# Inverses of the RWKV chunks applied ahead in batches, and a credit for small products, in a one-layer hybrid decoder step

## The chip, the cores and the metric

The kernel runs on one core of a Trainium2 chip. The metric is device time in microseconds (us) of one execution. TensorE (PE in the profile) multiplies, VectorE (DVE) and ScalarE (ACT) do elementwise work and empty PSUM, GpSimd (POOL) does little here, and SyncE (SP) issues most DMAs. The program is written with a tile framework: it records the operations, places the tiles in memory, sets the semaphores and orders each engine's instructions by a plan of its own. Around the part that is changed here, the order on PE is not the framework's: the kernel writes it out itself.

## The reference

One step of one layer: RWKV-7 time mixing beside dilated window attention, for a prompt of 1024 tokens and for 8 x 4 sample tokens. In outline:

```python
h = x @ w_in                                 # 1024 -> 9344 columns: r,k,v,lora | gates | q,k,v | branch gates
# RWKV-7, 8 heads of 64; per token t and head:
#   sa = S @ (-kk_t);  S = S * w_t + sa (kk_t*a_t)^T + v_t k_t^T;  o_t = S @ r_t
# attention: 3 groups (window 128/512/2048, dilation 1/4/16) x 4 heads x 128, merged by their softmax sums
mix = sigmoid(g_r) * (y_r @ w_oa) + sigmoid(g_a) * (y_a @ w_ob)
y = layer_norm(ALPHA * x + mix @ w_out)
```

Outputs are y, the new keys and values, the final RWKV states and the last projected rows.

## The kernel before

All large products are made in float32r with the operands split into a high and a low part, three matmuls for one. A projection of 128 columns (`project_steps`, its matmuls are L172) multiplies 2 halves of the inner dimension x 3 pieces of 352 tokens x 12 matmuls, 72 in all, into three PSUM banks of a pool `pj` that has four. A `consume` function then empties each bank. Weights come in halves by DMA (`wraw`), ACT makes the high part (`whi`, L162) and DVE the low part (`wlo`, L163).

The program has these stages. First x is transposed and the lora columns are projected. Then comes the RWKV stage, from some 75 us to some 600 us, which holds 12 projections for r, k and v and 23 of `fill`: gates whose results wait in DRAM (`zd`, `gd`). After it comes attention with its 36 projections, the first of them for the values (V, tile `v`), keys and queries of the first head; and then the two branch products and the last product with its layer norm.

The RWKV recurrence is worked in chunks of 64 tokens. A unit is a pair of heads (j) and half of the prompt (hf), so there are eight units of eight chunks. For each unit:

- `unit` prepares: `KR` holds, per chunk, kappa (the normalised key, scaled by the decay) and r; `BK` the b and k vectors; L370 makes the products of the two, masked by DVE into `AT`; L389 is the bonus; `W` takes v (L397), `BT` the transposed BK (L407), and L416 makes `R0`, the tokens' own part of the right-hand side.
- `inverse` inverts the 32 x 32 blocks of the triangular matrix of each chunk on DVE (L441, L444) between two trips through DRAM.
- `scan` joins two block inverses into that of the chunk (L467, L477, with copies by ACT), and then goes through the eight chunks one after another. A chunk before: L496 multiplies the state with kappa and r; DVE adds R0 (L498, tile `R`); L503 multiplies with the chunk's inverse; ACT copies the result with a minus sign into `W` (L504); L508 multiplies W with BT; DVE adds it to the scaled state (L511, two halves). Both state tiles alternate. After the chunks L519 makes the output `Ot`.
- `norm` is the group norm: 17 DVE operations with one by ACT between (L523 to L544), transposes (L548), an ACT copy (L550), two DVE operations (L551, L554) and the write of y to `yd` (L555).

What sets the order on PE is `run_streams`. It holds an imagined clock `now`. Four generators (scans, norms, inverses, units) yield after each group of small products with two numbers: what the group costs on PE and how long its successor has to wait. The first generator whose time has come gives the next group; if none is ready, a piece of a projection is issued, four matmuls of 352 columns, which the plan counts at 0.592 us. Before the change, small groups that are ready go one behind the other. When the projections of this stage are used up, only small groups are left to `run_streams`; the framework may put matmuls of the attention projections between them.

The tiles of the RWKV stage lie in a pool `rp` that is given up at its end (`rw_stack.close()`), and the attention tiles, `v` first, take its memory.

Of the kernel before, what the change touches and what calls it, by code (L numbers as in the profile page):

```python
# [32 lines left out]
D_PM, D_HOP, D_ST, D_GN, D_IN, D_WU = 0.53, 0.99, 1.54, 12.6, 11.0, 0.48  # L33
# [50 lines left out]
def tile_layer(ctx: ExitStack, tc: tile.TileContext, A: dict, O: list):  # L84
# [370 lines left out]
    def scan(j, hf, KR, AT, W, BT, R0, E, bon, st, Xd, blk, out):  # L455
# [8 lines left out]
        both = [quads[8 * p + n] for n in range(8) for p in range(2)]  # L464
        pm = ps("sc")
# [21 lines left out]

        Ot = mk(rp, [P, 4, P], "Ot", 2)
        for c in range(8):
            p, c2 = c % 2, c // 2  # L490
            u, v = slice(64 * (1 - p), 64 * (1 - p) + 64), slice(64 * p, 64 * p + 64)
            S0, S1 = st[c % 2], st[1 - c % 2]
            SD = mk(rp, [P, P], "SD", 1)
            S.activation(SD[:], S0[:], AF.Copy, scale=E[:, c, 64:65])  # L494
            pr = ps("sc")
            T.matmul(pr[:, 0:P], KR[:, c2, 2 * p : 2 * p + 2, :], S0[:], start=True, stop=True)  # L496
            R = mk(rp, [P, P], "R", 1)
            V.tensor_tensor(R[u], pr[u, 0:P], R0[u, c2, :], ALU.add)  # L498
            S.activation(Ot[v, c2, :], pr[v, 0:P], AF.Copy)
            yield (0.2, D_HOP)  # L500
            pu = ps("sc")
            for e in range(2):
                T.matmul(pu[u, 64 * e : 64 * e + 64], AT[u, e, c, u], R[u, 64 * e : 64 * e + 64], start=True, stop=True)  # L503
            S.activation(W[u, c, :], pu[u, 0:P], AF.Copy, scale=-1.0)  # L504
            yield 0.4, D_WU

            pS = ps("sc")
            T.matmul(pS[:, 0:P], BT[:, c, :], W[:, c, :], start=True, stop=True)  # L508
            for e in range(2):
                d = slice(64 * e, 64 * e + 64)  # L510
                V.scalar_tensor_tensor(S1[d, d], pS[d, d], E[d, c, 64:65], SD[d, d], ALU.mult, ALU.add)  # L511
            yield (0.2, D_ST)
# [187 lines left out]

    def run_streams():
        now, piece = 0.0, 72 * 0.148 / (6 * PIECE)
        streams, prods = [[0.0, scans()], [0.0, norms()], [0.0, inverses()], [0.0, units()]], products()
        while streams or prods:
            for x in streams:
                if x[0] <= now:
                    r = next(x[1], 0)
                    if r == 0:
                        streams.remove(x)
                        break  # L710
                    if r is not None:
                        now += r[0]
                        x[0] = now + r[1]
                        break
            else:
                if prods and next(prods, 0) == 0:
                    prods = None
                now += piece

# [704 lines left out]
```

## Time and profile before

| | |
|---|---|
| median of 3 runs | 1381.0 us (1380.83 to 1381.04) |
| profiled execution: its own time | 1381.54 us |
| its span, first to last instruction | 1379.8 us |
| PE busy | 1344.1 us (97%), 9809 matmul instructions |
| weight loads (PEld) | 1245.0 us (90%) |
| DVE busy | 804.0 us (58%) |
| ACT busy | 467.2 us (34%) |
| POOL busy | 67.2 us (5%) |
| projections, L172 | 5544 matmuls, busy 398.7 + 382.8 + 381.9 us in its three forms |

A matmul's row in a timeline gives start and duration, but matmuls overlap: the end includes the way of the result to PSUM. What a matmul costs the engine is therefore read from start to start of successive rows and not from its duration. "x4" is four instructions merged in one row; a float32 matmul that is not a transpose runs as two instructions. Idle time in square brackets counts only what lies behind the modelled end of the matmul before.

### The profile page before, as it was taken

To read this page: it belongs to the slowest core of one execution; us is meant where nothing else is said; L and a number is where in the kernel's file an instruction comes from. 1 tells how busy PE (TensorE), PEld (TensorE's weight loads), DVE (VectorE), ACT (ScalarE), POOL (GpSimd) and SP (SyncE) were. 2 spreads that over 40 slices of the span, in tenths; PEclk is the share of its full clock that TensorE was granted. 3 is DMA by queue.
4 is the path that set the end of the run, shared out by engine and by line. 5 is a ranking of instruction groups with operands and counts; after the bars stand their busy time and mean duration, and the time that the engine had idled before them with its cause. 6 is when DMAs were issued, how large, how long until landed. Compare 5 with 4: busy or idle time off the path is not lost.

```text
span 1379.8 us, 25342 instructions
## 1 busy us (share of the span) xinstructions
PE 1344.1 (97%) x9809; PEld 1245.0 (90%) x9809; DVE 804.0 (58%) x2203; ACT 467.2 (34%) x1089; POOL 67.2 (5%) x82
## 2 busy tenths in 40 slices
PE   7999999999999999999999999999999999899997
PEld 7998998898988889999999999999999998799786
DVE  4358767677867757441555275437542845665565
ACT  4333434444344444431332333233323234132211
POOL 0000000000000000000100000000000000015100
PEclk9999999999999999999999999999999999999999
DMA  6112222412322242336645355635554556795221
GB/s 216 55 47 73 58 82 72 110 37 75 88 59 75 74 110 79 91 94 123 136 106 132 84 141 115 131 93 140 114 123 115 133 122 153 230 287 170 82 103 68
DMA packets 340270, 151.62 MB, mean 110 GB/s; under 512 B 188928, under 2 KB 329622, under 8 KB 339894
## 3 DMA queue, kind: packets, MB, share of 16 engines
q1 hardware_dynamic: 241270, 129.68, 34.6%
q10 hardware_dynamic: 98880, 20.32, 7.4%
q8 instruction: 77, 1.26, 0.4%
q14 instruction: 43, 0.35, 0.1%
HBM read 110.68 MB, written 38.97 MB: 108 GB/s over the span
## 4 chain that ended last, share of the span: by engine, by line
PE 74%; DVE 14%; DMA 7%; issue 2%; ACT 2%; SPq 1%; DVEq 0%; ACTq 0%
PE pj L172 52%; PE pj L1378 7%; DVE tm L441 2%; DVE X L444 2%; PE o L932 2%; DMA cb<-cd 2%; PE s L895 2%; DMA wraw<-in_w_in_dram 1%; DVE wlo L163 1%; DVE o L1178 1%; PE t L915 1%; PE sc L503 1%; PE s L1014 1%; PE g L370 1%; DVE AT L377 1%
## 5 line engine op out<-in xcount | busy, mean ns | idle before, releaser
L172 PE MATMUL pj<-xhi,whi 128*128 128x352 f32 x1848 | 398.7, 337 | 5.0 <-ACT xhi L1245 3.0
L172 PE MATMUL pj<-xlo,whi 128*128 128x352 f32 x1848 | 382.8, 328 | 0.0
L172 PE MATMUL pj<-xhi,wlo 128*128 128x352 f32 x1848 | 381.9, 328 | 0.4 <-DVE wlo L163 0.4
L172 PEld LDWEIGHTS pj<-xhi,whi 128*128 128x128 f32 x1848 | 302.9, 189 | 21.7 <-issue 10.5
L172 PEld LDWEIGHTS pj<-xhi,wlo 128*128 128x128 f32 x1848 | 307.6, 189 | 3.6 <-issue 1.2
L172 PEld LDWEIGHTS pj<-xlo,whi 128*128 128x128 f32 x1848 | 307.9, 189 | 2.5 <-issue 0.4
L163 DVE TENSOR_TENSOR wlo<-wraw,whi 128x512 fp32r<-128x512 f32 x162 | 113.4, 701 | 84.0 <-ACT whi L162 83.3
L162 ACT ACTIVATE whi<-wraw 128x512 fp32r<-128x512 f32 x162 | 100.6, 625 | 146.6 <-PE pj L172 89.0
L905 ACT ACTIVATE Sm<-Sm,nm 128x128 f32<-128x128 f32 (+1 forms) x96 | 42.4, 442 | 102.7 <-DVE nm L902 102.7
L511 DVE SCALAR_TENSOR_TENSOR st<-sc,E,SD 64x64 f32<-64x64 f32 x128 | 36.2, 283 | 47.7 <-PE sc L508 46.2
L441 DVE TENSOR_TENSOR tm<-Y,X 128x60 f32<-128x60 f32 (+24 forms) x248 | 52.6, 212 | 6.3
L444 DVE TENSOR_TENSOR X<-X,tm 128x60 f32<-128x60 f32 (+24 forms) x248 | 52.0, 210 | 6.4
L1378 PE MATMUL pj<-wl,mh 128*128 128x512 f32 (+1 forms) x136 | 52.0, 382 | 0.0
L897 DVE CUSTOM_DVE_ANT_0 Sm<-s,cst 128x128 f32<-128x128 f32 (+1 forms) x96 | 29.2, 346 | 39.0 <-PE s L895 38.3
L494 ACT ACTIVATE SD<-st,E 128x128 f32<-128x128 f32 x64 | 25.6, 400 | 58.5 <-DVE st L511 58.5
L758 POOL TENSOR_TENSOR kvp<-vv,kv 128x512 f32<-128x512 f32 x16 | 19.7, 1233 | 514.3 <-DVE Ss L766 387.0
L932 PE MATMUL o<-PT,Vt 128*128 128x128 f32 x280 | 38.7, 276 | 0.8 <-ACT PT L919 0.8
L895 PE MATMUL s<-k,q 128*128 128x128 f32 (+1 forms) x192 | 37.8, 326 | 1.7 <-DVE ml L897 1.6
L820 ACT ACTIVATE k<-pj 128x352 f32<-128x352 f32 (+1 forms) x36 | 16.2, 454 | 67.5 <-PE pj L172 60.9
L932 PEld LDWEIGHTS o<-PT,Vt 128*128 128x128 f32 x280 | 36.4, 191 | 1.5 <-ACT PT L919 1.1
L503 PEld LDWEIGHTS sc<-R,AT 64*64 64x64 f32 x256 | 19.7, 134 | 18.4 <-DVE R L498 7.9
L299 ACT ACTIVATE zt<-pj,der 128x352 f32<-128x352 f32 x48 | 26.4, 551 | 27.9 <-PE pj L172 26.7
(314 smaller groups left out, 1719.1 us busy)
## 6 DMA issues: line engine op xcount, KB each, us to landing
wraw<-in_w_in_dram SPq DMA_DIRECT2D x146, 256.0 KB
gd<-zt SPq DMA_DIRECT2D x48, 176.0 KB
gt<-gd SPq DMA_DIRECT2D x48, 176.0 KB
vs<-bt ACTq DMA_DIRECT2D x48, 128.0 KB
kc<-in_cache_kv_g_dram SPq DMA_DIRECT2D x48, 128.0 KB
Vt<-vs ACTq DMA_DIRECT2D x12, 512.0 KB
cb<-cd SPq DMA_DIRECT2D x12, 512.0 KB
zd<-zt SPq DMA_DIRECT2D x24, 176.0 KB
```

The source lines that it names most:

```text
L162: S.activation(hi[:], raw[:], AF.Copy)
L163: V.tensor_tensor(lo[:], raw[:], hi.bitcast(F32)[:], ALU.subtract)
L172: T.matmul(out, w[wi][:, n % 4, :], x[:, n % 4, :], start=first and n == 0, stop=last and n == 11)
L441: V.tensor_tensor(tm, Y[:, r : r + 1, r + 1 : 32].to_broadcast([P, m, n]), X[:, 0:m, r : r + 1].to_broadcast([P, m, n]), ALU.mult)
L444: V.tensor_tensor(X[:, 0:m, r + 1 : 32], X[:, 0:m, r + 1 : 32], tm, ALU.subtract)
L503: T.matmul(pu[u, 64 * e : 64 * e + 64], AT[u, e, c, u], R[u, 64 * e : 64 * e + 64], start=True, stop=True)
L511: V.scalar_tensor_tensor(S1[d, d], pS[d, d], E[d, c, 64:65], SD[d, d], ALU.mult, ALU.add)
L895: T.matmul(r, qT[:, i * P : (i + 1) * P], kT[:, keys[i][0] * P : keys[i][0] * P + n], start=True, stop=True)
L897: V.tensor_tensor_reduce(out=Sm[:, i, 0:n], in0=r, in1=m3 if g == 2 else m12[:, 256 - n : 256], scale=1.0, scalar=NEG, op0=ALU.add, op1=AL ...
L905: S.activation(Sm[:, i, 0:n], Sm[:, i, 0:n], AF.Exp, scale=SCALE, bias=nm[:, x : x + 1], accum_out=ml[:, g, 1, i : i + 1])
L932: T.matmul(po[:, (i % 4) * P : (i % 4 + 1) * P], st["Vt"][:, kb_, :], PT[:, n * P : (n + 1) * P], start=m == 0, stop=m == len(keys[i]) - 1,)
L1378: T.matmul(pb[:], a[:, k], wk, start=x == 0, stop=x == len(prods) - 1)
```

## The change

Three things change, all in the RWKV stage.

First, the chunk's inverse is no longer applied inside the chain of chunks. At the start of `scan`, four PE transposes bring kappa of all chunks into `kT` (two ACT copies); after the inverses are joined, 16 matmuls of 64 x 64 multiply the inverse with kappa, and ACT writes the result, with a minus sign, back into KR (two copies); 16 more do the same for R0 (one copy). In a chunk, DVE's addition then writes W itself; the two matmuls of L503 and the copy of L504 are gone.

Second, `run_streams` counts the planned PE time of small groups in `small`. Once it has reached 1.0 us, the next thing issued is a piece of a projection, while there are any; each piece takes 0.592 off.

Third, three waiting times of the plan are other numbers: 0.9 for 0.53 after the joining steps, 1.25 for 0.99 after a chunk's first product, and 1.2 after the second batch.

```diff
 D_PN, D_KR, D_AT, D_G, D_W, D_INV, D_UP = 0.65, 1.81, 7.0, 0.2, 2.09, 0.9, 14.4
-D_PM, D_HOP, D_ST, D_GN, D_IN, D_WU = 0.53, 0.99, 1.54, 12.6, 11.0, 0.48
+D_PM, D_HOP, D_ST, D_GN, D_IN, D_U0 = 0.9, 1.25, 1.54, 12.6, 11.0, 1.2
+SMALL = 1.0
...
+        pk = ps("sc")
+        for c2 in range(4):
+            T.transpose(pk[:, c2 * P : (c2 + 1) * P], KR[:, c2, 1:3, :], ident)
+        kT = mk(rp, [P, 4, P], "t", 6)
+        for p in range(2):
+            u, v = slice(64 * (1 - p), 64 * (1 - p) + 64), slice(64 * p, 64 * p + 64)
+            S.activation(kT[u], pk[v, :].rearrange("p (a b) -> p a b", a=4), AF.Copy)
+        yield (0.45, 0.5)
         pm = ps("sc")
...
+        chunks = [(c // 2, c % 2, e) for c2 in range(4) for e in range(2) for c in (2 * c2, 2 * c2 + 1)]
+        pk = [ps("sc") for p in range(2)]
+        for c2, p, e in chunks:
+            u = slice(64 * (1 - p), 64 * (1 - p) + 64)
+            T.matmul(
+                pk[p][64 * e : 64 * e + 64, 64 * c2 : 64 * c2 + 64],
+                kT[u, c2, 64 * e : 64 * e + 64], AT[u, e, 2 * c2 + p, u], start=True, stop=True,
+            )
+        for p in range(2):
+            S.activation(KR[:, :, 1 + p, :], pk[p][:, 0:256].rearrange("p (a b) -> p a b", a=4), AF.Copy, scale=-1.0)
+        yield (1.0, D_PM)
+        pu = ps("sc")
+        for c2, p, e in chunks:
+            u = slice(64 * (1 - p), 64 * (1 - p) + 64)
+            T.matmul(
+                pu[u, c2 * P + 64 * e : c2 * P + 64 * e + 64],
+                AT[u, e, 2 * c2 + p, u], R0[u, c2, 64 * e : 64 * e + 64], start=True, stop=True,
+            )
+        S.activation(R0[:], pu.rearrange("p (a b) -> p a b", a=4), AF.Copy, scale=-1.0)
+        yield (1.0, D_U0)
...
             T.matmul(pr[:, 0:P], KR[:, c2, 2 * p : 2 * p + 2, :], S0[:], start=True, stop=True)
-            R = mk(rp, [P, P], "R", 1)
-            V.tensor_tensor(R[u], pr[u, 0:P], R0[u, c2, :], ALU.add)
+            V.tensor_tensor(W[u, c, :], pr[u, 0:P], R0[u, c2, :], ALU.add)
             S.activation(Ot[v, c2, :], pr[v, 0:P], AF.Copy)
             yield (0.2, D_HOP)
-            pu = ps("sc")
-            for e in range(2):
-                T.matmul(pu[u, 64 * e : 64 * e + 64], AT[u, e, c, u], R[u, 64 * e : 64 * e + 64], start=True, stop=True)
-            S.activation(W[u, c, :], pu[u, 0:P], AF.Copy, scale=-1.0)
-            yield 0.4, D_WU
...
         while streams or prods:
-            for x in streams:
...
-            else:
+            if (small >= SMALL and prods) or not step():
                 if prods and next(prods, 0) == 0:
                     prods = None
                 now += piece
+                small = max(0.0, small - piece)
```

The lines below shift: L496, L508, L519 and L548 become L528, L534, L545 and L574; L172 becomes L173 and L820 L854. The new transposes are L469, the new batches L503 and L513.

The order on PE in the middle of the first unit's scan, before, over one chunk (`sc` are PSUM tiles of the chain, `pj` banks of projections, `st` the state):

```order
L496 MATMUL sc_2072<-st_79_481,KR_885 128x128
L172 MATMUL pj_2022<-xlo_9_87,whi_2026 128x352 x4
L172 MATMUL pj_2023<-xhi_7_85,whi_2026 128x352 x4
L503 MATMUL sc_2091<-R_2074,AT_976 64x64 x2
L172 MATMUL pj_2023<-xhi_7_85,wlo_2027 128x352 x4
L508 MATMUL sc_2105<-W_1017,BT_1029 128x128
L172 MATMUL pj_2023<-xlo_9_87,whi_2026 128x352 x4
L172 MATMUL pj_2021<-xhi_8_86,whi_2121 128x352 x4
L172 MATMUL pj_2021<-xhi_8_86,wlo_2122 128x352 x4
```

And now:

```order
L528 MATMUL sc_2054<-st_80_482,KR_885 128x128
L173 MATMUL pj_1989<-xhi_7_85,wlo_1993 128x352 x4
L173 MATMUL pj_1989<-xlo_9_87,whi_1992 128x352 x4
L173 MATMUL pj_1987<-xhi_8_86,whi_2080 128x352 x4
L534 MATMUL sc_2088<-W_1029,BT_1041 128x128
L173 MATMUL pj_1987<-xhi_8_86,wlo_2081 128x352 x4
L173 MATMUL pj_1987<-xlo_10_88,whi_2080 128x352 x4
L173 MATMUL pj_1988<-xhi_8_86,whi_2080 128x352 x4
```

Two, one and three pieces between the three products of a chunk have become three and three between two.

The order on PE at the end of the last unit's scan, before (`pj_7366` to `pj_7368` and `pj_7543` are projections of `fill`, of which this one and two more are still to come):

```order
L508 MATMUL sc_7460<-W_6329,BT_6348 128x128
L172 MATMUL pj_7367<-xhi_8_86,whi_7435 128x352 x4
L172 MATMUL pj_7367<-xhi_8_86,wlo_7436 128x352 x4
L172 MATMUL pj_7367<-xlo_10_88,whi_7435 128x352 x4
L519 MATMUL g_7481<-W_6329,AT_6236 64x64 x16
L559 MATMUL g_7499<-ident_69,st_687_3644 128x128
L172 MATMUL pj_7368<-xhi_8_86,whi_7435 128x352 x4
L172 MATMUL pj_7368<-xhi_8_86,wlo_7436 128x352 x4
L172 MATMUL pj_7368<-xlo_10_88,whi_7435 128x352 x4
L172 MATMUL pj_7543<-xhi_7_85,whi_7548 128x352 x4
```

And now (`pj_7841` to `pj_7843` are the three banks of the first attention projection, V; `pj_7933` and `pj_7934` are the first two of the second, K; L574 are the transposes of the last unit's norm):

```order
L534 MATMUL sc_7746<-W_6792,BT_6832 128x128
L545 MATMUL g_7750<-W_6792,AT_6680 64x64 x16
L585 MATMUL g_7768<-ident_69,st_648_3699 128x128
L173 MATMUL pj_7843<-xlo_10_88,whi_7888 128x352 x3
L173 MATMUL pj_7933<-xhi_7_85,whi_7938 128x352 x4
L173 MATMUL pj_7933<-xhi_7_85,wlo_7939 128x352 x4
L173 MATMUL pj_7933<-xlo_9_87,whi_7938 128x352 x4
L173 MATMUL pj_7933<-xhi_8_86,whi_7980 128x352 x4
L173 MATMUL pj_7933<-xhi_8_86,wlo_7981 128x352 x4
L173 MATMUL pj_7933<-xlo_10_88,whi_7980 128x352 x4
L574 MATMUL g_7795<-ident_69,Ot_7669 128x128 x4
L173 MATMUL pj_7934<-xhi_7_85,whi_7938 128x352 x4
```

All projections of `fill` now stand ahead of the last scan's chunks, and between these stand V's 72 matmuls, three to eleven at a time; behind the scan, 27 matmuls stand ahead of the norm's transposes.

The order on ACT at the same place, now, with what each instruction waits for (`v` is the first attention tile, in the memory of the RWKV pool):

```order
L563 ACTIVATE sz_7778<-Ot_7669 128x512 [waits DVE_49]
L576 ACTIVATE Ot_7669<-g_7795,prm_339 128x512 [waits DVE_49,PE_49,Activation_49]
L854 ACTIVATE v_7904<-pj_7841 128x352 [waits DMAHW3_49,DMAHW2_49,DMAHW4_49,DMAHW1_49,DMAHW5_49,DMAHW0_49,DMAHW6_49,DVE_49,DMAHW7_49,Activation_49,Pool_49]
L854 ACTIVATE v_7904<-pj_7842 128x352
L854 ACTIVATE v_7904<-pj_7843 128x320
L854 ACTIVATE k_7996<-pj_7933 128x352
L897 DMA vs_1456_8157<-bt_8156 32x32x32 [waits DVE_49]
```

V's first bank is emptied behind the last unit's norm; one of the DMA counts that it waits for is that of the last unit's write to `yd` (L581). Before, the same instruction waited for the last write of `fill` to `zd` instead. From the first attention matmul on, the order on PE is the same in both kernels.

More of the change, by code (lines that the diff above doesn't have):

```diff
@@ L701, in run_streams, with step @@
     def run_streams():
-        now, piece = 0.0, 72 * 0.148 / (6 * PIECE)
+        now, piece, small = 0.0, 72 * 0.148 / (6 * PIECE), 0.0
         streams, prods = [[0.0, scans()], [0.0, norms()], [0.0, inverses()], [0.0, units()]], products()
-        while streams or prods:
+        def step():
+            nonlocal now, small
             for x in streams:
@@ L709, in run_streams @@
                         streams.remove(x)
-                        break
+                        return True
                     if r is not None:
                         now += r[0]
+                        small += r[0]
                         x[0] = now + r[1]
-                        break
-            else:
+                        return True
+            return False
+        while streams or prods:
+            if (small >= SMALL and prods) or not step():
                 if prods and next(prods, 0) == 0:
```

## The prediction

> **What bounds the kernel now.** I read the page's first part, the busy time by stretches, PE's waits, and then PE's timeline with DVE's, ACT's and SP's beside it.
>
> ```profile
> PE 1344.1 (97%) x9809; PEld 1245.0 (90%) x9809; DVE 804.0 (58%) x2203; ACT 467.2 (34%) x1089; POOL 67.2 (5%) x82
> ```
>
> ```profile
> 400.00:450.00 50.00, 48.58 (x406) 43.93 (x405) 40.99 (x149) 19.57 (x46) 1.31 (x3) 1.00 0.25 68
> ```
>
> ```profile
> PE g L370 <- DVE AT L377: 2.7, 8, 1.0
> PE g L407 <- ACT W L400: 2.6, 6, 0.4
> PE sc L503 <- DVE R L498: 2.3, 6, 0.6
> ```
>
> PE is the bound, over the whole run and in the RWKV stage: of 50 us from 400 on it is busy 48.58, DVE 40.99, ACT 19.57. So time is saved where PE has less to issue or waits less. These three waits, the longest of this stage (total, times, longest), make 7.6 us of idle time; the rest is matmuls, whose price I read from start to start:
>
> ```profile
> 596.39 0.38 PE L496 MATMUL sc<-st,KR 128*128 128x128 f32 x2
> ...
> 597.26 0.81 PE L172 MATMUL pj<-xhi,wlo 128*128 128x352 f32 x4
> 598.00 0.44 PE L503 MATMUL sc<-R,AT 64*64 64x64 f32 x4
> 598.37 0.91 PE L172 MATMUL pj<-xlo,whi 128*128 128x352 f32 x4
> 599.12 0.38 PE L508 MATMUL sc<-W,BT 128*128 128x128 f32 x2
> ...
> 601.36 1.20 PE L519 MATMUL g<-W,AT 128*64 128x64 f32 x32
> 602.49 0.33 PE L559 MATMUL g<-ident,st 128*128 128x128 f32 x1
> ...
> 616.24 0.81 PE L172 MATMUL pj<-xhi,whi 128*128 128x352 f32 x4
> 616.88 0.60 PE L548 MATMUL g<-ident,Ot 128*128 128x128 f32 x4
> 617.24 0.89 PE L172 MATMUL pj<-xhi,wlo 128*128 128x352 f32 x4
> 617.97 0.81 PE L172 MATMUL pj<-xlo,whi 128*128 128x352 f32 x4
> ```
>
> A piece of four projection matmuls costs 0.64 (616.24 to 616.88), 0.16 each. With L503 between, two pieces take 1.86 (597.26 to 599.12): the group of L503 costs 1.86 - 1.28 = 0.58, although it multiplies only two 64 x 64 blocks. Part of this lies in the pieces beside it, which take 0.74 and 0.75 where the array changes its shape.
>
> **The change: removed.** 64 groups of L503 (eight units, eight chunks), 64 x 0.58 = 37.1 us of PE. The copies of L504 were on ACT, which is idle most of the time; DVE's addition stays, with another destination.
>
> **Added.** Per unit four transposes, like L548's: 616.24 to 617.97 is 1.73, less 1.28, so 0.45. And two batches of 16 products of 64 x 64. L416 is one such batch, with 32 passes:
>
> ```profile
> 134.90 0.80 PE L172 MATMUL pj<-xhi,wlo 128*128 128x352 f32 x4
> 135.63 1.15 PE L416 MATMUL g<-W,AT 64*64 64x64 f32 x32
> 136.71 0.92 PE L172 MATMUL pj<-xlo,whi 128*128 128x352 f32 x4
> 137.46 0.80 PE L172 MATMUL pj<-xhi,whi 128*128 128x352 f32 x4
> ```
>
> 134.90 to 137.46 is 2.56, less 1.28: 1.28 a batch. Eight units: 8 x (0.45 + 2 x 1.28) = 24.1. PE's work falls by 37.1 - 24.1 = 13.0 us. L416's passes take 34 ns each (1.08 for 32) against 93 in L503 (0.37 for four): its neighbours use different rows of the array and run in pairs. The new batches alternate the rows in the same manner.
>
> The Trainium skill speaks against this for the second batch: "TensorEngine Tiling (Array Packing)", section Restrictions and Gotchas, says that different row tiles cannot access the same PSUM bank at the same time, and that batch writes both halves into one bank. By the rule its passes would run one after another, and the sum would be worse by the 15 us that the last rival works out. L416 also writes one bank from both halves, and its 1.08 us shows the pairs, so the trace does not bear the rule out.
>
> ACT gets five copies per unit for eight: no cost, since it is busy 19.57 of 50 us; only if a copy came late would PE wait for it, and between the groups stand one to three pieces (0.64 to 1.9 us).
>
> **Waits in the middle of the stage.** After a chunk's first product the sum is ready 0.70 later and after its last the state 1.0 later, if DVE is free:
>
> ```profile
> 596.81 0.28 DVE L498 TENSOR_TENSOR R<-sc,R 64x128 f32<-64x128 f32 x1 [1.54 <-PE sc L496]
> ...
> 599.54 0.28 DVE L511 SCALAR_TENSOR_TENSOR st<-sc,E,SD 64x64 f32<-64x64 f32 x1 [1.59 <-PE sc L508]
> ...
> 600.37 0.29 DVE L511 SCALAR_TENSOR_TENSOR st<-sc,E,SD 64x64 f32<-64x64 f32 x1
> 602.60 0.69 DVE L523 TENSOR_TENSOR Ot<-Ot,g 128x512 f32<-128x512 f32 x1 [1.94 <-PE g L519]
> 603.21 0.51 DVE L199 SCALAR_TENSOR_TENSOR zt<-zt,pj 128x352 f32<-128x352 f32 x1
> ...
> 609.67 0.69 DVE L544 TENSOR_TENSOR Ot<-Ot,nt 128x512 f32<-128x512 f32 x1
> ...
> 615.71 0.52 DVE L199 SCALAR_TENSOR_TENSOR zt<-zt,pj 128x352 f32<-128x352 f32 x1 [2.08 <-DMA zd<-zt]
> ...
> 618.33 0.69 DVE L551 TENSOR_TENSOR Ot<-Ot,bon 128x512 f32<-128x512 f32 x1 [0.54 <-ACT Ot L550]
> ...
> 619.37 0.68 DVE L554 TENSOR_TENSOR Ot<-Ot,sz 128x512 f32<-128x512 f32 x1
> ```
>
> (L496 starts at 596.39, so the sum is there at 597.09; L508 at 599.12, the first half at 599.82, the second 0.28 later if nothing of `fill` comes between.) Now three pieces, 1.9 us, stand behind each of the two, so DVE may be late by almost a microsecond without PE noticing. L503's 2.3 us go; so does most of L407's 2.6, since L407 no longer follows L503 directly and pieces stand around it. L370's second half stood one piece behind the first, and waited for DVE's mask:
>
> ```profile
> 121.87 0.90 PE L172 MATMUL pj<-xlo,whi 128*128 128x352 f32 x4
> 123.82 0.48 PE L370 MATMUL g<-KR,BK 64*128 64x128 f32 x2 [1.05 <-DVE AT L377]
> ```
>
> The credit puts two pieces there: 0.64 of some 1.2 us goes. From start to start these waits are longer than the list has them (121.87 to 123.82 is 1.95, against 0.75 for a piece at a change of shape). I take 8 us less waiting; at least 4 (L503 and most of L407), at most 13 (all 7.6, and up to a quarter of a microsecond behind the modelled end in each of the 20 cases).
>
> **What it costs: the cover of the end.** Before, more than two projections of `fill` (over 20 us) ran behind the last scan and hid the last norm. Now they are used up ahead of the last scan's chunks. V's 72 matmuls cover these chunks: a pair of L496 with a piece takes 0.87 (596.39 to 597.26), so with three or four matmuls 0.71 or 0.87, with five 1.03, against 0.75 and 1.05 needed with the handing over. That loses about 1 us in eight chunks. Then comes the stop. Counted from the last output product: DVE starts 1.24 later (601.36 to 602.60) and needs 602.60 to 610.36, 7.8, less two `zt` of 0.5 that go with `fill`, 6.7; the norm's transposes can start at 7.9. PE has 1.2 for the product and the state, and 27 matmuls of 0.16: 5.6. It waits 2.4. After the transposes all four `pj` banks are full, three with V and one with K. V cannot be emptied before y has landed in DRAM:
>
> ```profile
> 617.52 0.78 ACT L550 ACTIVATE Ot<-g,prm 128x512 f32<-128x512 f32 x1
> ```
>
> ```profile
> 638.21 0.47 ACT L820 ACTIVATE v<-pj 128x352 f32<-128x352 f32 x1 [1.43 <-PE pj L172]
> ```
>
> ```profile
> 613.65 2.93 SPq L200 DMA_DIRECT2D zd<-zt  x2
> ...
> 620.08 0.32 SPq L555 DMA_DIRECT2D yd<-Ot  x1
> ```
>
> Transposes to ACT 0.64 (616.88 to 617.52), 0.78, two DVE operations 0.69 + 0.68, a write of 2.06 (the first of the two `zd` writes, issued at 613.65, freed its tile at 615.71; `yd` gets 512 columns for 352, so no less), 0.47 for V's first bank, some 0.2 of handing over: 5.5 from the transposes' start, of which these fill 0.4. PE stands 5.1 us. After a stop like that the clock falls:
>
> ```profile
> 1176.42 0.95 PE L172 MATMUL pj<-xhi,whi 128*128 128x352 f32 x3 [3.03 <-ACT xhi L1245]
> ...
> 1178.13 1.38 PE L172 MATMUL pj<-xhi,wlo 128*128 128x352 f32 x4
> 1179.30 1.22 PE L172 MATMUL pj<-xlo,whi 128*128 128x352 f32 x4
> ```
>
> After 3.03 us idle a piece took 1.17 (1178.13 to 1179.30) instead of 0.64, 0.53 more; three such pieces cost 1.6. Attention's first loads start after the same release and have 24 matmuls, 3.9 us, less lead: 0 to 4, I take 1. Sum: 1 + 2.4 + 5.1 + 1.6 + 1 = 11 us; at least 6 (no fall of the clock, the norm a microsecond quicker, no late load), at most 19 (DVE's weight splittings, 0.7 each, in the norm's chain and in the chunks, and 4 of loads).
>
> **Sum.** -13.0 - 8 + 11 = -10. From the profiled execution's 1381.5 (span 1379.8, 1.7 around it; the median is 0.5 lower): 1371.5 us.
>
> **Rivals.** Within 0.2% (2.8 us) I call it the same, about what a measurement of this kernel can tell.
>
> - The end costs little, 6 us: -13 - 8 + 6 gives 1366.5. For it speaks that V's matmuls are already spread over the chunks; against it, the order and the wait on the write are fixed. 0.2.
> - The waits only move: DVE, busy 41 of 50 us, stays late, 2 us saved, and the end costs 12: -13 - 2 + 12 gives 1378.5, with 14 at the end 1380.5, the same. 0.15.
> - The other side: attention starts late. ACT takes its queue in order, and its second emptying of K stands behind DMA issues that wait for the state's load:
>
> ```profile
> 654.92 0.79 ACT L820 ACTIVATE k<-pj 128x352 f32<-128x352 f32 x2 [6.55 <-DMA Ss<-in_state_rwkv_wkv_dram]
> ```
>
>   ACT stood 6.55 us there while PE had projections to issue. With 3.9 us less lead and V's next weights split behind it, PE may now wait the 6.55 and as long again for the weights behind: the end costs 11 + 13 = 24, 1384.5, slower. It decides from an end of 24 us on (13 + 8 + 2.8). Against it: those 6.55 us cost PE nothing before. 0.1.
> - The first batch's pairs write the same columns of the array. If its passes ran like L503's four (0.37), a batch took 8 x 0.37 = 3.0 for 1.08, eight of them +15: 1386.5, slower. L416 speaks against it. 0.05. The rule of the Trainium skill on banks, named above, would do the same to the second batch.
>
> That the credit would not part the small groups is ruled out by the order. The forecast has 0.5. Faster: 0.5 + 0.2 = 0.7; same 0.15; slower 0.1 + 0.05 = 0.15. The likeliest case alone is 1366 to 1378, by its bounds for waits and end. The range, 1364 to 1381, leaves out the slower cases and the tip of the first rival.
>
> **What would show it.** After the change L503's 256 passes should be gone from the chain, the two batches stand with 1.1 us for 32 passes, and the waits of L370, L407 and the chain's products fall below 4 us together. PE should reach the first attention scores some 10 us earlier than before:
>
> ```profile
> 669.74 0.82 PE L895 MATMUL s<-k,q 128*128 128x128 f32 x4
> ```
>  Between the last scan and V's emptying there should be two stops of PE, near 2.4 and 5.1 us, and half the clock after them. If batches take 2 us or more, or PE stops again when the second V projection starts, the forecast is wrong.

## The result

The changed kernel takes 1382.88 us (median of 14 runs, 1379.04 to 1388.47), the kernel before 1380.24 us (14 runs, 1378.52 to 1382.03): a ratio of 1.0024, with a 95% interval from 1.0013 to 1.0035. The change is slower by about a quarter of a per cent. The forecast was 1371.5 us, with a range that ended at 1381: it missed by 11 us and on the wrong side.

The first part of the profile after, and the 50 us from 400 on, which the prediction shows for the kernel before:

```profile
PE 1338.5 (97%) x10097; PEld 1245.3 (90%) x10097; DVE 803.8 (58%) x2203; ACT 469.2 (34%) x1065; POOL 65.7 (5%) x82
```

```profile
400.00:450.00 50.00, 48.81 (x453) 45.09 (x452) 35.69 (x135) 21.37 (x45) 0.99 (x3) 1.00 0.26 72
```

PE is busy 5.6 us less, and nothing came of it. PE's timeline tells where to look. The order on PE from the first attention scores on is the same in both kernels; they started at 669.74 us before, and should have started some 10 us earlier:

```profile
671.71 0.82 PE L929 MATMUL s<-k,q 128*128 128x128 f32 x4
```

So the expected gain is missing already here, in the RWKV stage. The products did get cheaper, as PE's timeline of one unit shows (L469 the transposes of kappa, L503 the first batch, L513 the second):

```profile
338.76 0.60 PE L469 MATMUL sc<-ident,KR 128*128 128x128 f32 x4
339.11 0.89 PE L173 MATMUL pj<-xhi,whi 128*128 128x352 f32 x4
...
344.15 0.69 PE L503 MATMUL sc<-AT,t 64*64 64x64 f32 x32
344.77 0.92 PE L173 MATMUL pj<-xlo,whi 128*128 128x352 f32 x4
...
348.20 1.15 PE L513 MATMUL sc<-R,AT 64*64 64x64 f32 x32
349.28 0.91 PE L173 MATMUL pj<-xlo,whi 128*128 128x352 f32 x4
```

The transposes stand for 0.35 us (338.76 to 339.11), the first batch's 32 passes for 0.62 (344.15 to 344.77), the second's for 1.08 (348.20 to 349.28). With what the projection pieces beside them take longer they cost 0.44, 0.82 and 1.28 us. The transposes and the second batch cost what was forecast, the first batch less.

What took the gain away are waits. The list of waits for PE, from 76 to 605 us, shortly ahead of the last scan, after (the columns are total, times, longest, in us):

```profile
PE sc L528 <- DVE st L537: 3.2, 7, 0.6
PE g L295 <- DVE nt L318: 2.4, 2, 1.7
PE sc L534 <- DVE W L529: 1.6, 4, 0.8
PE g L371 <- ACT Ot L576: 1.4, 3, 0.5
PE g L371 <- DVE AT L378: 1.1, 2, 0.8
```

Before, the longest in this list were L370's, L407's and L503's, 7.6 us together; they are mostly gone, and others have come in their place: the chunk's two products, L528 (the old L496) and L534 (the old L508), now wait for DVE. And behind the last scan stand the two stops that were forecast; PE's rows, with SP's and ACT's between:

```profile
638.37 0.93 PE L574 MATMUL g<-ident,Ot 128*128 128x128 f32 x4 [2.29 <-DVE Ot L570]
641.64 0.32 SPq L581 DMA_DIRECT2D yd<-Ot  x1
643.93 1.15 ACT L854 ACTIVATE v<-pj 128x352 f32<-128x352 f32 x3 [3.77 <-DMA yd<-Ot]
644.45 1.54 PE L173 MATMUL pj<-xhi,whi 128*128 128x352 f32 x4 [5.15 <-ACT v L854]
645.79 1.38 PE L173 MATMUL pj<-xhi,wlo 128*128 128x352 f32 x4
646.96 1.38 PE L173 MATMUL pj<-xlo,whi 128*128 128x352 f32 x4
648.14 1.11 PE L173 MATMUL pj<-xhi,whi 128*128 128x352 f32 x4
```

**The account.** The list counts only idle time behind a matmul's modelled end, so I sort PE's time from start to start. From the first unit's first product to the first scores each projection matmul counts 0.161 us. A group of small products between two projection pieces counts from start to start less the pieces; the least that such a group took in these traces is its price (0.22 for L528, 0.57 for the old L503, 0.82 and 1.28 for the batches), groups directly behind one another count as the sum of their prices, and what lies above the price is waiting.

| us | before | after |
|---|---|---|
| small products at their price | 164.7 | 146.8 |
| waits ahead of the last scan | 13.1 | 18.4 |
| waits from the last scan on | 0.0 | 11.6 |
| projections, and all that is left | 415.1 | 416.2 |
| sum, first unit to first scores | 593.0 | 593.1 |

In the row of the projections after, 2.1 us are half clock: the four pieces from 644.45 on took 1.34, 1.17, 1.18 and 0.94 instead of 0.645. So 17.9 us were saved and all of them lost again: 5 more in the middle, 14 at the end. How the middle splits into work and waiting hangs on these prices: the profile's own list of idle time, up to 605 us, has 9.6 us before and 9.7 after. Work and waiting together, 12.6 us less in the middle where 21 were forecast, do not hang on them. (The medians differ by 2.6 us, these two executions by 0.1 in this part. The first unit started at 76.8 us in the one and at 78.7 in the other, behind a part that both have alike; in the runs below it started anywhere from 76.4 to 78.9. The part behind the first scores, with one order on PE, took 710.1 us before and 708.6 after, and 706.7 to 713.3 in the runs below that leave POOL as it was: what the account finds shows in a run's time only within some microseconds.)

### The profile page after: what moved, and what is told of

Its sections match the earlier page's. It is cut to its first block, busy times and chain, and to the rows that moved or that the text cites. A ratio compares the mean times of both kernels' runs of the same rounds, so it can differ in the third digit from the quotient of the medians.

```text
span 1380.3 us, 25914 instructions
## 1 busy us (share of the span) xinstructions
PE 1338.5 (97%) x10097; PEld 1245.3 (90%) x10097; DVE 803.8 (58%) x2203; ACT 469.2 (34%) x1065; POOL 65.7 (5%) x82
## 4 chain that ended last, share of the span: by engine, by line
PE 84%; DVE 10%; DMA 3%; issue 1%; SPq 1%; ACT 1%; ACTq 0%; DVEq 0%
PE pj L173 61%; PE pj L1412 7%; DVE tm L442 2%; PE o L966 2%; DVE X L445 2%; PE s L929 2%; PE g L371 1%; PE t L949 1%; PE s L1048 1%; PE sc L528 1%; DVE st L537 1%; DVE wlo L164 1%; PE sc L534 1%; PE g L545 1%; SPq L1108 1%
## 5 line engine op out<-in xcount | busy, mean ns | idle before, releaser
L173 PE MATMUL pj<-xhi,whi 128*128 128x352 f32 x1848 | 400.5, 337 | 10.6 <-ACT v L854 5.2
L173 PE MATMUL pj<-xhi,wlo 128*128 128x352 f32 x1848 | 386.4, 330 | 0.0
L173 PE MATMUL pj<-xlo,whi 128*128 128x352 f32 x1848 | 385.0, 329 | 0.0
L173 PEld LDWEIGHTS pj<-xhi,whi 128*128 128x128 f32 x1848 | 304.4, 190 | 29.2 <-issue 11.7
L173 PEld LDWEIGHTS pj<-xhi,wlo 128*128 128x128 f32 x1848 | 308.6, 190 | 5.3 <-issue 3.5
L173 PEld LDWEIGHTS pj<-xlo,whi 128*128 128x128 f32 x1848 | 308.9, 190 | 3.6 <-issue 2.1
L164 DVE TENSOR_TENSOR wlo<-wraw,whi 128x512 fp32r<-128x512 f32 x162 | 112.9, 697 | 85.3 <-ACT whi L163 84.4
L442 DVE TENSOR_TENSOR tm<-Y,X 128x60 f32<-128x60 f32 (+24 forms) x248 | 53.0, 214 | 6.2
L445 DVE TENSOR_TENSOR X<-X,tm 128x60 f32<-128x60 f32 (+24 forms) x248 | 52.3, 211 | 6.3
L259 DVE SCALAR_TENSOR_TENSOR m<-pj,prm,m 128x351 f32<-128x351 f32 (+1 forms) x39 | 22.2, 570 | 37.0 <-ACT m L258 36.8
L854 ACT ACTIVATE k<-pj 128x352 f32<-128x352 f32 (+1 forms) x36 | 16.4, 455 | 66.2 <-PE pj L173 63.2
L530 ACT ACTIVATE Ot<-sc 64x128 f32<-64x128 f32 x64 | 17.4, 272 | 60.7 <-DVE W L529 60.4
```

The source lines that it names most:

```text
L164: V.tensor_tensor(lo[:], raw[:], hi.bitcast(F32)[:], ALU.subtract)
L173: T.matmul(out, w[wi][:, n % 4, :], x[:, n % 4, :], start=first and n == 0, stop=last and n == 11)
L442: V.tensor_tensor(tm, Y[:, r : r + 1, r + 1 : 32].to_broadcast([P, m, n]), X[:, 0:m, r : r + 1].to_broadcast([P, m, n]), ALU.mult)
L445: V.tensor_tensor(X[:, 0:m, r + 1 : 32], X[:, 0:m, r + 1 : 32], tm, ALU.subtract)
```

## Experiments

All times are medians, all ratios against the kernel before run beside them. "Waits" are those of the account, ahead of the last scan and from it on; the small products take 147 to 148 us in each run with the batches and 163 to 165 in those without. Each account is of one profiled execution; it lay 3.3 us under the median of its runs in e2 and e3 and 3.0 over it in e4, and at most 4.6 off (e11) in the others that have an account.

### Credit and batches apart (e1 to e4)

The first theory was that all was lost at the end: the credit parts the small groups with projection pieces, so each unit uses up more projections, and none are left for the last norm.

```diff
-SMALL = 1.0                                              # the change
+SMALL = 1e9                                              # e1, e2
+D_PM, D_HOP, D_ST, D_GN, D_IN, D_U0 = 0.53, 0.99, 1.54, 12.6, 11.0, 1.2   # e2
+SMALL = 2.0                                              # e4
```

> The change with SMALL at a thousand million, so that the credit never holds a small product back; batches and waits (D_PM 0.9, D_HOP 1.25) as in the change. Theory 'spent cover': the batches save PE about 16 us (64 groups of 0.57 out; 8 x (0.44 + 0.82 + 1.28) in), the credit lets each unit use up more projection matmuls, and that is why nothing covers the end. Without it the last scan ends with over 300 projection matmuls still to issue, as before, and the two stops of PE (2.3 and 5.2 us) and the half clock behind them are gone: 1364 us (1361 to 1369). Rival 'the wait moves': it is the chain of two products a chunk that waits for DVE, whatever stands ahead of it, and without the credit small products stand directly behind one another: waits in the middle rise by 5 to 15 us, 1370 to 1381.

> As e1, but the dispatcher's waits for the scan's setup and the chunk's sum at the values of before (D_PM 0.53, D_HOP 0.99): two pieces instead of three behind a chunk's first product. 'Spent cover': units run through faster still, the end has more cover than it needs, and the time is that of e1 within 3 us (1362 to 1370). 'The wait moves': DVE has 0.64 us less for the sum in each of 64 chunks and is later than that in part of them: 5 to 20 us above e1.

e3 has the products of before, and only the dispatcher of the change (`step`, `small`, SMALL = 1.0).

> The kernel before, with L503 in its chunks and its own waits, but with the change's dispatcher and its credit of 1.0. 'Spent cover': the end loses its cover here too (only 160 matmuls behind the last norm's transposes, of which the fill has none): V's emptying stops PE for about 5 us and the half clock costs about 5 more, the waits in the middle fall by at most 3: 1385 to 1391, slower than before by 0.4 to 0.8%. Rival 'the credit saves waits': 1372 to 1378.

> The change with a credit of 2.0 instead of 1.0. 119 instead of 66 matmuls in the last scan's chunks, 42 instead of 27 between its outputs and the last norm's transposes, 175 instead of 156 behind. 'Spent cover': the chunks' waits of some 3 us and the stop of 2.3 us go, the stop for V's emptying (5.2) and half clock (5) stay: 1374 to 1378. 'The wait moves': as the change, 1380 to 1384.

| | us | ratio, 95% interval | waits ahead | waits at the end |
|---|---|---|---|---|
| before | 1380.0 | | 13.1 | 0.0 |
| change | 1382.9 | 1.0024 (1.0013 to 1.0035) | 18.4 | 11.6 |
| e1, batches, no credit | 1385.9 | 1.0041 (1.0029 to 1.0053) | 35.0 | 0.0 |
| e2, the same, old waits | 1387.6 | 1.0064 (1.0042 to 1.0087) | 35.2 | 0.1 |
| e3, credit alone | 1383.3 | 1.0025 (1.0015 to 1.0036) | 10.6 | 5.4 |
| e4, batches, credit 2.0 | 1380.5 | 1.0004 (0.9995 to 1.0014) | 23.8 | 6.0 |

(For e3 and e4 the stop for V's emptying, 4.5 and 2.1, lies between projections and is added to the last column; for e4 1.3 more for a `zt` tile.)

"Spent cover" as the only cause falls with e1: the end has its cover, its stops are gone, and the kernel is slower still. e2, with one piece less behind each sum, has the waits of e1, and its time cannot be told from e1's by these intervals. Each part of the change alone is slower than before, and so is the sum. The credit does what it is for in part: it takes 17 us of waits out of the middle (35.0 to 18.4) and puts 12 to 14 at the end. e4 is the best mixture, equal to the kernel before. That leaves open why the batches, which take 18 us off PE, raise the waits ahead of the last scan from 13 to 35.

### Is it the order in DVE's queue? (e5, e7, e12)

In the change one of the waits looks like this in PE's and DVE's timeline (L442 and L445 are the elimination in `inverse` for the next unit, L164 splits a weight tile, L529 is the chunk's sum):

```profile
378.70 0.46 PE L528 MATMUL sc<-st,KR 128*128 128x128 f32 x2 [0.36 <-DVE st L537]
...
379.90 0.23 DVE L445 TENSOR_TENSOR X<-X,tm 128x72 f32<-128x72 f32 x1
380.17 0.23 DVE L442 TENSOR_TENSOR tm<-Y,X 128x68 f32<-128x68 f32 x1
380.31 0.69 DVE L164 TENSOR_TENSOR wlo<-wraw,whi 128x512 fp32r<-128x512 f32 x1
381.03 0.28 DVE L529 TENSOR_TENSOR W<-sc,R 64x128 f32<-64x128 f32 x1
381.37 0.49 PE L534 MATMUL sc<-W,BT 128*128 128x128 f32 x2 [0.29 <-DVE W L529]
```

A sum that finds DVE free starts 0.42 us after its product (the least lag of all); this one started 2.33 after it (378.70 to 381.03), and DVE was busy all that time with the elimination of the next unit and a weight tile. For all sums and states up to 600 us, the lag beyond 0.70 adds up to 50 us in the change and 24 before, and DVE is busy in some 48 and 23 of them. So the sum stands in a queue. Two edits move it forward in that queue and leave the order on PE alone (but for one matmul in e5).

```diff
+            with tc.high_priority():                     # e5; e7 with SMALL = 1e9
-            V.tensor_tensor(W[u, c, :], pr[u, 0:P], R0[u, c2, :], ALU.add)
+                V.tensor_tensor(W[u, c, :], pr[u, 0:P], R0[u, c2, :], ALU.add)
...                                                       # and the state's two operations
-            V.tensor_tensor(tm, Y[...], X[...], ALU.mult)
+            tc.keep_in_program_order(V.tensor_tensor(tm, Y[...], X[...], ALU.mult))   # e12, instead
```

> The change, with the chunk's two kinds of DVE operations (L529's sum and L537's state) issued at high priority, so that DVE's queue takes them ahead of the elimination of the next unit (L442, L445) and the weights' splitting (L164) where both are ready; the order on PE is the change's but for one matmul. Theory 'DVE's queue': PE waits in the chunks because the sum and the state stand in DVE's queue behind other units' work; the 13 us of waits before L528 and L534 outside the last scan fall by a half or more: 1373 to 1378. Rival 'the hand-over itself': the semaphores, the product's latency and the ACT copy of the state set the wait, and the order on DVE does not matter: 1381 to 1385. The end (stops of 2.3 and 5.2 us) stays in both.

> e1 (no credit, batches) with the high priority of e5. 'DVE's queue': of e1's 35 us of waits, those before the chunk's products (some 20) fall by a half or more, the end has cover: 1372 to 1378. 'The hand-over itself': 1384 to 1388, as e1.

> The change, with each row of the elimination kept behind all DVE operations that the dispatcher issued before it (the order on PE is the change's; in DVE's queue more of the gaps between chunk operations hold one or four elimination operations instead of six or more). 'DVE's queue': waits before L528 and L534 fall by a quarter to a half: 1376 to 1380. 'The hand-over itself': 1381 to 1385. If the inverse then comes late for its scan, waits appear before L477: 1385 to 1395.

| | us | ratio, 95% interval | waits ahead | waits at the end |
|---|---|---|---|---|
| e5 | 1382.9 | 1.0018 (1.0006 to 1.0030) | 17.9 | 12.0 |
| e7 | 1387.5 | 1.0057 (1.0040 to 1.0074) | 33.8 in all | |
| e12 | 1382.7 | 1.0022 (1.0008 to 1.0035) | 17.7 | 11.4 |

None changed the time. e5 and e7 say little against the queue, since the priority moved hardly an operation (the lag adds up to 48.5 us instead of 50.3); perhaps the plan that orders DVE had preferred the chunk already where both are ready. e12 says more. There the lag beyond 0.70 fell from 50 to 30 us and the waits of chunk groups that stand alone between pieces fell from 13.4 to 7.1 us, but the waits in sum did not fall; they went to other groups. The list of waits in e12 over the same stretch (L478 waits for `T1`, which needs the inverse):

```profile
PE sc L478 <- DVE T L465: 2.1, 1, 2.1
PE g L295 <- DVE X L446: 1.4, 1, 1.4
PE g L371 <- DVE AT L378: 1.3, 2, 1.1
```

### Without the elimination (e9, e10, e11)

If DVE simply has too much to do, order does not help, and leaving work out does.

```diff
         for r in range(31):
             m, n = r // 4 + 1, 31 - r
+            if r % 2:
+                yield (0.0, D_INV)
+            continue
             tm = mk(rp, [P, 80], "tm", 2)[:, 0 : m * n].rearrange("p (a b) -> p a b", a=m)
```

> The change without the elimination (L442 and L445, 62 DVE operations of 0.2 us a unit, left out: the inverses' 32 x 32 blocks stay the identity, and the output is not the reference's); the order on PE is the change's. After e5, where the priority moved hardly an operation in DVE's queue, the theory 'DVE's queue' says: the chunk's sum and state start late because elimination stands ahead of them in DVE's queue. The 18 us of PE's waits ahead of the last scan fall to 6 or less, the end's stops stay: 1369 us (1366 to 1373). Rival 'the hand-over itself': 1381 to 1385.

> The kernel before without the elimination, as e9 (leaves out the same operations). 'DVE's queue': its 13 us of waits fall to 4 or less: 1371 (1368 to 1374). 'The hand-over itself': 1379 to 1382. The gap between e9 and this one tells what the change is worth where DVE is free: by the theory about -18 for the products, +16 for the end, so -5 to +2.

> e1 (batches, no credit) without the elimination, as e9. 'DVE's queue' and 'spent cover' together: e1's 35 us of waits fall to 6 or less and the end has its cover: 1357 (1353 to 1363), more than 10 us below e9 and e10. 'The hand-over itself': 1383 to 1388. If the end's stops cost nothing of themselves, it comes out within 3 us of e9.

| | us | ratio, 95% interval | waits ahead | waits at the end |
|---|---|---|---|---|
| e9, change without elimination | 1367.5 | 0.9907 (0.9885 to 0.9929) | 4.2 | 11.3 |
| e10, before without it | 1372.8 | 0.9944 (0.9925 to 0.9964) | 9.1 | 0.0 |
| e11, e1 without it | 1366.1 | 0.9898 (0.9876 to 0.9921) | 17.3 | 0.0 |

The elimination costs PE 14 us of waits in the change (18.4 to 4.2), 18 without the credit (35.0 to 17.3), but only 4 in the kernel before (13.1 to 9.1). Busy time in the stretch of one unit in which the elimination runs beside chunks, from the change, then the kernel before, then e9 at the same place of the program (columns: length, then busy PE, PEld, DVE, ACT, POOL, clock, DMA):

```profile
369.50:391.00 21.50, 20.36 (x129) 19.07 (x129) 19.54 (x87) 8.31 (x19) 0.20 (x1) 1.00 0.23 71
```

```profile
342.60:363.40 20.80, 20.19 (x130) 18.37 (x130) 18.66 (x78) 8.13 (x22) 0.00 (x0) 1.00 0.21 70
```

```profile
361.90:383.50 21.60, 21.60 (x140) 21.08 (x140) 9.68 (x30) 9.64 (x21) 0.32 (x2) 1.00 0.25 80
```

DVE is busy 91% of such a stretch in the change (19.54 of 21.50), 90% before, and 45% in e9. So for 20 to 28 us of each unit DVE has hardly a gap left. PE's starts of the chunks' first products show it, in the change, before, and e9 (L531 there is L528):

```profile
378.70 0.46 PE L528 MATMUL sc<-st,KR 128*128 128x128 f32 x2 [0.36 <-DVE st L537]
383.63 0.38 PE L528 MATMUL sc<-st,KR 128*128 128x128 f32 x2
388.63 0.46 PE L528 MATMUL sc<-st,KR 128*128 128x128 f32 x2 [0.49 <-DVE st L537]
```

```profile
348.65 0.38 PE L496 MATMUL sc<-st,KR 128*128 128x128 f32 x2
353.54 0.38 PE L496 MATMUL sc<-st,KR 128*128 128x128 f32 x2
358.40 0.38 PE L496 MATMUL sc<-st,KR 128*128 128x128 f32 x2
```

```profile
366.25 0.38 PE L531 MATMUL sc<-st,KR 128*128 128x128 f32 x2
370.58 0.38 PE L531 MATMUL sc<-st,KR 128*128 128x128 f32 x2
374.87 0.39 PE L531 MATMUL sc<-st,KR 128*128 128x128 f32 x2
```

A chunk beside the elimination takes 4.93 and 5.00 us in the change and 4.89 and 4.86 before, with six pieces in each; without the elimination (e9) it takes 4.33 and 4.29. Before, this was still PE's own pace: six pieces of 0.645, two products of 0.22 and L503's 0.57 are 4.88, and these rows have no stop (the next chunk, from 358.40 on, lost some 0.8). In the change PE's part is 4.31, and the chunk takes what DVE needs, nearly as long as with L503. DVE was just quick enough for the old chunk and is not for the new one. The 0.57 us that each chunk no longer spends on L503 is there only where DVE is free. With some four such chunks in each of seven units that makes about 16 us of the saving that cannot be had, near the 14 that e9 shows. Whether the elimination would cost PE as much if it were spread over the whole of a unit, some 65 us, was not tried.

Side by side, e9 and e10 tell what the change does where DVE is free. From the first unit to the first scores e10 took 587.4 us and e9 578.3, 9.1 less; work and waits in the middle are 22.8 less, near the forecast's 21. (The medians are only 5.2 us apart; the part behind the first scores took 711.8 us in e9 and 707.7 in e10.)

e11 holds the other half. It was expected at 1357, since it has both a free DVE and a covered end. Its waits ahead are 17.3, not 6: without the credit, small groups stand directly behind one another and wait for each other's results (L371, the bonus, the copies between the two joins), elimination or not. That is 13 us more than e9, against 11.3 at e9's end. The credit moves waits from the middle to the end, at nearly one for one.

### The elimination on another engine (e6, e8, e13 to e18)

e6 frees DVE of the weights' splitting, e8 does the same with e4's credit and e5's priority, and e13 to e18 put the elimination on POOL, which is busy 5% of the time.

```diff
-        V.tensor_tensor(lo[:], raw[:], hi.bitcast(F32)[:], ALU.subtract)      # L164
+        G.tensor_tensor(lo[:], raw[:], hi.bitcast(F32)[:], ALU.subtract)      # e6, e8
...
-            V.tensor_tensor(tm, Y[...], X[...], ALU.mult)                     # and the same for X
+            G.tensor_tensor(tm, Y[...], X[...], ALU.mult)                     # e13 to e18
...
-            V.transpose(T1[u : u + 32], AT[...])                              # L464
+            tc.keep_in_program_order(V.transpose(T1[u : u + 32], AT[...]))    # e17, e18
```

> The change, with the subtraction that splits a weight tile (L164, 0.68 us on DVE, some 60 of them in this stage) on POOL instead of DVE. 'DVE's queue': DVE has 40 us less to do between 76 and 600 us, its busy share in the chunks falls from about 0.7 to 0.6, waits before L528 and L534 fall by a half: 1374 to 1379. Rival 'the hand-over itself': 1381 to 1385. If POOL's operation (1.1 us for 128x352 elsewhere) holds DVE up or brings weights late, the time rises: 1385 to 1395.

> Batches, credit 2.0 (e4), high priority (e5) and the weights' splitting on POOL (e6) together. 'DVE's queue': waits in the chunks nearly gone, and the cover of the end as in e4: 1363 to 1370, below both kernels. 'The hand-over itself': 1378 to 1384.

e6 took 1421.4 us (ratio 1.0299, 1.0277 to 1.0321), e8 1416.9 (1.0272, 1.0254 to 1.0291). POOL did hold DVE up. Groups on DVE from 76 to 600 us, the change and then e6 (count, busy us, mean ns of one):

```profile
L442 DVE TENSOR_TENSOR tm<-Y,X 128x60 f32<-128x60 f32 (+24 forms) x248 | 53.0, 214 | 6.2
L445 DVE TENSOR_TENSOR X<-X,tm 128x60 f32<-128x60 f32 (+24 forms) x248 | 52.3, 211 | 6.3
```

```profile
L445 DVE TENSOR_TENSOR X<-X,tm 128x60 f32<-128x60 f32 (+24 forms) x237 | 61.8, 261 | 6.2
L442 DVE TENSOR_TENSOR tm<-Y,X 128x60 f32<-128x60 f32 (+24 forms) x238 | 54.6, 230 | 6.0
L529 DVE TENSOR_TENSOR W<-sc,R 64x128 f32<-64x128 f32 x51 | 14.7, 288 | 31.3 <-PE sc L528 30.5
```

L445 and L442, whose two inputs both lie in SBUF, went from 211 to 261 and from 214 to 230 ns, while L529, which takes one from PSUM, stayed at 288. The Trainium skill, "SBUF — State Buffer", section Who interferes with whom, says that a DVE instruction with two SBUF inputs contends with a GpSimd instruction that reads SBUF, and one with at most one SBUF input does not; these rows agree. Longer elimination makes some 2 us a unit (31 x 0.050 + 31 x 0.016), 16 in all, of the 38 by which e6 is slower than the change; the rest was not followed up.

> The change, with the elimination (L442, L445) on POOL instead of DVE; nothing is left out, and the order on PE is the change's. Theory 'DVE full': in some 22 us of each unit the elimination's 13 us bring DVE to a busy share of about 1, and there DVE, not PE, sets the time of a chunk; so what the change takes off PE comes back as waits. With the elimination on POOL it goes as without it (e9): 1368 to 1373. Rival 'POOL holds DVE up': POOL's operations make DVE's longer, as in e6, or bring the inverse late (waits before L477): 1383 to 1400.

> As e13, with a credit of 2.0. 'DVE full' and 'spent cover': the 9 us that the end is shorter with that credit (e4) come on top, less some 5 us of waits between small products that stand closer: 1364 to 1370, below e13 and below the kernel before. 'POOL holds DVE up': 1381 to 1398.

> The kernel before, with the elimination on POOL. 'DVE full': as e10, 1372 to 1376, and so above e13 by 2 to 6. 'POOL holds DVE up': 1381 to 1395.

> e1 (no credit) with the elimination on POOL. As e11: 1366 to 1371; 17 us of waits between small products that follow one another directly, none at the end. 'POOL holds DVE up': 1386 to 1400.

e13 took 1440.9 us, e14 1448.6, e15 1449.7 and e16 1446.4 (ratios 1.0437 to 1.0497, each known to 0.0022): 60 to 70 us slower, the kernel before (e15) too. In e13 the chunks came at 4.3 us without a wait, except at a few places where PE stopped for 6 to 14 us. At one of them PE's and DVE's timelines show why:

```profile
335.90 0.44 DVE L464 STREAM_TRANSPOSE T<-AT 32x256 f32<-32x256 f32 x1 [7.07 <-DMA AT<-Xd]
...
338.23 0.29 DVE L529 TENSOR_TENSOR W<-sc,R 64x128 f32<-64x128 f32 x1
338.58 0.80 PE L534 MATMUL sc<-W,BT 128*128 128x128 f32 x2 [6.28 <-DVE W L529]
```

L464 needs the next unit's inverse back from DRAM, and stood in DVE's queue ahead of this unit's L529. e17 and e18 put it behind.

> As e13 (the change, elimination on POOL), and the transposes of T1 (L464), which wait for the inverse and in e13 stood in DVE's queue ahead of another unit's chunks (stops of 6 to 14 us), kept behind all DVE operations that the dispatcher issued before them: all chunks of a unit stand ahead of the next unit's transposes. 'DVE full': the five stops of e13 go, its other chunks already came without waits; POOL needs 24 to 27 us a unit for the elimination, as DVE did between other work: 1368 to 1374. 'The inverse is late': POOL's elimination ends too late for its scan, the stops only move to L477: 1385 to 1420.

> As e17, with the credit of 2.0, which leaves more projections for the end: 'DVE full' with 'spent cover': 1362 to 1369, below e17 by about the 4 to 9 us by which e4's end was shorter. 'The inverse is late': 1385 to 1420, and more than e17, since the units follow one another more closely.

e17 took 1442.4 us (1.0466, 1.0438 to 1.0495), e18 1439.2 (1.0424, 1.0403 to 1.0445). PE's waits in e17 and SP's queue:

```profile
PE sc L477 <- DVE T L464: 15.0, 6, 5.4
PE g L343 <- DVE Ot L549: 13.7, 3, 6.0
PE g L371 <- DVE AT L378: 13.4, 1, 13.4
...
PE sc L528 <- DVE st L537: 0.6, 2, 0.3
PE sc L534 <- DVE W L529: 0.5, 1, 0.5
```

```profile
SPq L449 <- POOL X L445: 40.0, 3, 17.2
```

The chunks' own waits are nearly gone with the elimination off DVE, 1.1 us against 4.8 in the same list of the change. In that, e17 bears out what e9 showed. But the time did not follow: the stops moved to L477, as the rival said, and to others. One cause can be read: the writes of the inverse (L449) stand in SP's queue until POOL is done, 40 us in all, and the weights' loads and the `zd` writes stand behind them. The stops also slow what runs behind them: the mean granted clock from the first unit to the first scores was 0.95 in e17, 0.99 in the change and 1.00 before. How much of the 60 us each of these is, and whether the elimination on POOL can be planned so that it pays, stays open. Apart from e9 to e11, which leave the elimination out and are no kernels to use, no version here beats the kernel before; e4 equals it.

## Why the prediction was wrong

By its own terms, forecast and measured (us):

| term | forecast | measured |
|---|---|---|
| PE work, -37.1 + 24.1 | -13.0 | -17.9 |
| waits in the middle | -8 (4 to 13 less) | +5.3 |
| end | +11 (6 to 19) | +13.7 |
| sum | -10 | +1 |

**The step that failed** is "Waits in the middle of the stage", where it says that "three pieces, 1.9 us, stand behind each of the two, so DVE may be late by almost a microsecond without PE noticing". The sum's start was taken from one chunk, at 596 us (0.42 after its product), in the last unit, which has no elimination beside it; the mean of DVE's busy time, 41 of 50 us, was taken for what holds in every stretch. It does not: over the 20 to 28 us in which the next unit is eliminated DVE is at 90%, and a chunk there lasts 4.9 to 5.0 us without L503 too, where PE's part is 4.31. The waits named before (L370, L407, L503) went for the most part, as forecast. Those of L528 and L534 came, and e9 shows what they hang on: without the elimination the waits in the middle would have been 4.2, and the term -9 against the 13.1 of before, or -5 against e10's 9.1. Where DVE is free, the forecast's sum nearly holds, 9.1 us less from e10 to e9 for 10, though its terms err both ways (work -17.9 for -13, waits -4.9 for -8, the end some 13 for 11).

The rival "the waits only move: DVE, busy 41 of 50 us, stays late" had the mechanism. It gave 1378.5 to 1380.5 and a chance of 0.15. It was too low in the waits (2 less, for 5 more).

**PE's work** came out 5 us better. The transposes cost 0.44 (forecast 0.45), the second batch 1.28 as forecast, the first 0.82 instead of 1.28, and L503's groups 0.57 instead of 0.58. That makes -16.2 by the forecast's own sum; the other 1.7 us were not followed. The prediction puts the longer pieces beside L503 down to a change of the array's shape. That is not all of it: behind L548's transposes, 128x128 like the projections, a piece took 0.73 as well (617.24 to 617.97).

**The end** was right in its mechanism and in its two stops: 2.29 us forecast as 2.4, 5.15 forecast as 5.1. Two sizes were off. The last scan's chunks lost 3.1 us, not 1 (each of L528 and L534 waited 0.1 to 0.3 with three to five matmuls of V ahead). The half clock lasted longer than after the earlier stop from which it was sized, 10.1 us:

```profile
638.60:648.70 10.10, 4.95 (x18) 4.55 (x17) 2.73 (x4) 2.28 (x5) 0.00 (x0) 0.50 0.42 105
```

It began with the transposes, behind the first stop, and ran over the second, so only some 4 us of it had work in it: 2.1 us lost in the pieces and up to 0.9 at the transposes, against 1.6. Attention's late loads (+1) did not show as a stop of PE.

**The other rivals.** "The end costs little" did not happen. "Attention starts late behind ACT's queue" did not either: the first scores came at 671.71, and no new stop stands between V's emptying and them. The batches did not run serially: 34 ns a pass in L513 (1.08 for 32), as in L416. There the rule of the Trainium skill on row tiles and one PSUM bank, "TensorEngine Tiling (Array Packing)", Restrictions and Gotchas, would have had the second batch, whose halves share a bank, take as long per pass as the old L503's 93 ns; the trace does not agree.

## What to carry to other kernels

A wait is worth what the engine behind it has free in that stretch, so read the busy share in the window where the wait stands, not over a round 50 us. Work taken off the bound engine comes back as waits wherever a second engine is nearly full, and one run without that engine's other work shows it. And pieces that are spent to cover waits early are missing at the end: without the elimination (e11 and e9) the credit took 13 us of waits out of the middle and put 11 at the end.

## What the runs showed of the hardware

- 32 passes of 64 x 64 took 0.62 us in L503, which uses both halves of the rows and, by turns, both halves of the columns, each row half with a bank of its own, and 1.08 in L513 and L416, where each row half has one column half and both share a bank. Which of the two differences matters was not tried. In L416 the passes of the two row halves mostly started 6 to 7 ns apart and the next pair 51 to 52 later, so a pair came every 59 ns; the two passes of a product in the old L503, which use one row half, started 58 to 59 apart.
- The same 128x512 subtraction took 0.69 us on DVE and 1.33 on POOL in this stage, an elimination step of up to 80 columns 0.21 and 0.31 to 0.32 (e13):

```profile
L164 POOL TENSOR_TENSOR wlo<-wraw,whi 128x512 fp32r<-128x512 f32 x60 | 79.8, 1330 | 403.5 <-ACT whi L163 390.9 <-PE sc L528 7.2 <-DMA X<-in_cst_dram 5.4
```
